# Moving the cross-attention's memory products ahead of the state recurrence in a hybrid encoder layer

## The chip, the cores and the metric

The kernel runs on one core of a Trainium2 chip. The metric is the device time of one execution in microseconds. The core has five engines with their own queues: PE (TensorE, matmuls and, as PEld, weight loads), DVE (VectorE), ACT (ScalarE), POOL (GpSimd) and SP (SyncE). In this kernel SP issues most of the DMAs and ACT the others.

## The reference

One layer of an encoder on x (2048 x 1024), with memory tokens mem (256 x 1024), all in float32:

```python
u = _rms_norm(h, norm_mix_g[l])
proj = u @ w_in[l]
hy = _short_conv_centred(proj[..., :HY_COLS], hy_conv_w[l], hy_conv_b[l])
spec = _hyena_filter_spectrum(L, ...)
y_hy = _group_rms_norm(_hyena(hy, spec, hy_skip[l]), hy_norm_g[l], HYENA_GROUPS)
qk = jax.nn.silu(_short_conv_centred(proj[..., HY_COLS:off], ml_conv_w[l], ml_conv_b[l]))
y_ml = _mlstm_bidirectional(qk[..., :D_MLSTM], qk[..., D_MLSTM:], v, o, gates, ml_gate_b[l])
y_ml = _group_rms_norm(y_ml, ml_norm_g[l], MLSTM_HEADS)
h = h + jnp.concatenate([y_hy, y_ml], axis=-1) @ w_out[l]
h = h + _cross_attention(_rms_norm(h, norm_x_g[l]), _rms_norm(mem, norm_mem_g[l]),
                         xa_wq[l], xa_wk[l], xa_wv[l], xa_wo[l])
h = h + jnp.square(jax.nn.relu(_rms_norm(h, norm_ff_g[l]) @ ff_w1[l])) @ ff_w2[l]
return _rms_norm(h, final_norm_g)
```

`_hyena` applies two long convolutions one after the other, each by a transform, a product with the filter's spectrum and an inverse transform over all 2048 positions. `_mlstm_bidirectional` is a recurrence over chunks of the sequence, once forwards and once backwards, for four heads of 128; the carried state of a head is a 128 x 128 matrix and a vector of 128.

## The kernel before

**Products in three parts.** A float32 product is made of three fast ones (`mm3`, L340 to L342): each operand is split into a rounded part and a remainder (`split`, L345: a cast on ACT, a subtraction on DVE). Weights come through `weights` (L374 for blocks of 256 columns, L369 for blocks of 1024): 256 KB land in a staging tile `wn` (three of these), are split into `wh` and `wl` (two of each), and `stream` keeps one item of the list `self.items` loading ahead. Each item is 1 MB.

**The input projection.** `w_in` is taken in ten blocks of 256 columns with the columns on the partitions (`sweep`: products of 512 positions, then the short convolution, then a transpose back) and in four blocks with the positions on the partitions (`natural`: products of 256 columns). Both walk over two halves of the sequence, `hf` 0 and 1. Blocks 0 and 1 of `natural` are v, blocks 2 and 3 are the output gate, block 3 also holds the 16 gate columns. Results go to DRAM (`hy`, `qt`, `kt`, `kn`, `vd`, `od`, `gt`).

**The convolution.** `hyena` first transforms z (`f1`), then for each of the two convolutions runs 16 frequency blocks (L845 the filter's response, L918 the transform, L876 the way back) and eight steps of the inverse transform (L177 and L188 side by side through `beside`, with `e2`), in the second convolution followed by the group norm on POOL and DVE and the store `yh`. It reads and writes its intermediate values in DRAM (`zs`, `zg`).

**The memory products.** Attention's queries and keys, and its values and output matrix, are joined beforehand: `memproj` makes, for each of eight items (four heads of xa_wk, four of xa_wv), a projection of mem (`project`, products of 256 columns), and from it either `keys` (with a 1 MB block of xa_wq, into `gd`) or `values` (with a block of xa_wo, into `vw`). mem's operand lies in four tiles `mt` that `prep_mem` fills.

**The states.** The backward recurrence needs a state ahead of each chunk of 128: `backward` makes 15 of them, from chunk 15 down. A step (`update`) scales v by the gate weights (POOL, L1078, tile `ve`), multiplies it with k (TensorE, L1082), adds the decayed old state (DVE, L1088, tile `cb`) and stores it to `cbd` (L1107); k and v come by L1064 and L1070. Each of these loads and stores is 256 KB. `far_states` makes the first eight inside the convolution, in a small pool with one `ve` and two `cb`; `mlstm` loads the eighth back (`old_state`, L1094) and makes the other seven in its own pool, then goes through the 16 chunks forwards (scores L1175, products with v L1213 and with the states L1215, and the forward update, L1082 again with DVE as its engine). At its start it loads the gate rows (L1142, eight DMAs).

**The order.** Everything is written as generators that yield a rough weight, and `weave(a, b, wa, wb)` lets two of them advance in proportion. `among` puts one step of a second generator after every so many of the first. The list of `program` is:

```python
weave(p.hyena(hs),
      chain(s, p.sweep(range(4, 10), 1, True), p.natural(1, (3, 0, 1, 2), lambda: p.prep_x(0)),
            p.natural(0, (3,)), among(p.sweep(range(4, 10), 0, False), p.gates(), 3),
            among(chain(p.natural(0, (0, 1), p.prep_mem, 2), take(n, 5)), p.far_states(), 1)),
      279, 499)
m = p.mlstm(ms)
weave(n, take(m, 13), 85, 75)
```

`n` is `memproj`. A scheduler with its own timing then sets each engine's queue from this order and from priorities; some instructions are pinned with `keep_in_program_order`. Each engine runs its queue in order. Pools are stacked, and a pool's space is given on only when its last readers are done.

Of the kernel before, what the change touches and what calls it, by code (L numbers as in the profile page):

```python
# [10 lines left out]
F32 = mybir.dt.float32  # L11
# [9 lines left out]
D = 1024  # L21
# [112 lines left out]
class Prog:  # L134
# [247 lines left out]
            cur = nxt  # L382
        yield cur

    NAT_AT = {0: 2}

    def inproj_open(self, es):
        nc, tc, a = self.nc, self.tc, self.a
        self.d_hy = self.dram("hy", (3, L, CH))
        self.d_qt = self.dram("qt", (4, 128, L))  # L390
        self.d_kt = self.dram("kt", (4, 128, L))
        self.d_kn = self.dram("kn", (L, CH))
        self.d_vd = self.dram("vd", (L, CH))
        self.d_od = self.dram("od", (L, CH))
        self.d_gt = self.dram("gt", (L, 16))
        sb = self.isb = es.enter_context(tc.tile_pool(name="i_sb", bufs=1))
        self.xh = sb.tile([128, 8, 1024], F32R, name="xh")
        self.xl = sb.tile([128, 8, 1024], F32R, name="xl")
        small = sb.tile([128, 448], F32, name="small")
        self.carry = small[:, 0:340].rearrange("p (c t) -> p c t", c=20)  # L400
        self.rx, self.rm = small[:, 340:356], small[:, 356:358]
        win = a["w_in"][0]
        tr = [(win[:, 256 * c:256 * c + 256], 256) for c in range(10)]
        nat = [(win[:, 2560 + 256 * c:2816 + 256 * c + 16 * (c == 3)], 256 + 16 * (c == 3)) for c in range(4)]
        hs = [slice(256 * h, 256 * h + 256) for h in range(4)]
        first = [(a[w][0][:, h], 256) for w in ("xa_wk", "xa_wv") for h in hs]
        second = [(a["xa_wq_t"][h, :], 1024) for h in hs] + [(a["xa_wo"][0][h, :], 1024) for h in hs]
        mem = first[:1]
        for i in range(8):
            mem += ([nat[self.NAT_AT[i]]] if i in self.NAT_AT else []) + first[i + 1:i + 2] + second[i:i + 1]  # L410
        items = tr[:4] * 2 + tr[4:] + [nat[c] for c in (3, 0, 1, 2, 3)] + tr[4:] + nat[:2] + mem
        self.items = items

    def inv_rms(self, dst, src):
# [166 lines left out]
    def prep_x(self, hf):  # L581
        self.prepq = chain(self.x_chunk(2 * hf), self.x_chunk(2 * hf + 1))

    def prep_mem(self):
        sb = self.isb
        self.memt = [[sb.tile([128, 1088], F32R, tag=tag, name="mt", bufs=2)[:, 0:D].rearrange("p (k t) -> p k t", k=4)
                      for tag in ("P", "cv")] for h in range(2)]

        def load(h):
            t = sb.tile([128, D], F32, tag="xn", name="xt", bufs=2).rearrange("p (k t) -> p k t", k=4)  # L590
            self.nc.sync.dma_start(out=t, in_=self.a["mem_t"].rearrange("(k p) t -> p k t", p=128)[:, 4 * h:4 * h + 4])
            return t

        def halves():
            xs = [load(h) for h in range(2)]
            rb = self.spread(self.diagonal(self.rm))
            for h in range(2):
                self.scaled(xs[h], 4 * h, self.g_mem, rb, *self.memt[h])
                yield
        self.prepq = halves()  # L600

    def memproj(self):
        nc, sb = self.nc, self.isb
        gd = self.dram("gd", (2, 128, 8, 512))
        vw = self.dram("vw", (4, 128, 8, 256))
        self.pop(2)
        mt = self.memt

        def project():
            wh, wl = next(self.wst)  # L610
            p = self.mm().rearrange("p (k t) -> p k t", k=2)
            for m in range(2):
                ms = slice(128 * m, 128 * m + 128)
                for k in range(8):
                    self.mm3(p[:, m], wh[:, k, ms], wl[:, k, ms], mt[k // 4][0][:, k % 4], mt[k // 4][1][:, k % 4], k == 0, k == 7)
            t = sb.tile([128, 2, 2, 256], F32R, tag="xn", name="kt", bufs=2)
            self.split(t[:, 0], t[:, 1], p)
            return t

# [25 lines left out]
                    o = staged(p.rearrange("p (i t) -> p i t", i=2))  # L645
                    nc.scalar.dma_start(out=vw[2 * d:2 * d + 2, :, 2 * h + mt].rearrange("i p c -> p i c"), in_=o)

        t = project()
        for i in range(8):
            if i in self.NAT_AT:  # L650
                yield from self.natural(0, (self.NAT_AT[i],))
            yield 11
            nxt = project() if i < 7 else None
            (keys if i < 4 else values)(i % 4, t)
            t = nxt

    def sweep(self, cols, hf, first, after=None):
        nc, a, sb = self.nc, self.a, self.isb
# [429 lines left out]
                nc.vector.scalar_tensor_tensor(new[:, h], old[:, h], DC[:, r + h:r + h + 1],  # L1088
                                               pc[:, 129 * i:129 * i + 129], ALU.mult, ALU.add)

    def old_state(self, sb, n):
        t = sb.tile([128, 4, 129], F32, tag="cf", name="cb", bufs=3)
        cbd = self.dram("cbd", (15, 128, 516))
        self.nc.sync.dma_start(out=t.rearrange("d h e -> d (h e)"), in_=cbd[n - 1])  # L1094
        return t

    def backward(self, sb, first, last, old, pin=None, lean=False):
        kn = self.dram("kn", (L, CH)).rearrange("(n s) c -> s n c", s=128)
        cbd = self.dram("cbd", (15, 128, 516))
# [8 lines left out]
            old = new  # L1108
        yield 3

    def far_states(self):
        with self.tc.tile_pool(name="m_b", bufs=1, side="right") as sb:
            yield from self.backward(sb, 15, 7, None, self.tc.keep_in_program_order, True)

    def mlstm(self, es):
        nc, tc, a = self.nc, self.tc, self.a
# [22 lines left out]
        for s in range(2):  # L1139
# [1 line left out]
            for q in range(4):  # L1141
                nc.sync.dma_start(out=t[32 * q:32 * q + 32], in_=by_half[s])  # L1142
# [721 lines left out]
def chain(*gens):  # L1864
    for g in gens:
        yield from g
# [20 lines left out]
def program(p):  # L1887
    with ExitStack() as ms:
        with ExitStack() as es:
            p.inproj_open(es)  # L1890
            p.filters_open()
            p.prepq = p.x_first()
            p.pop()
            s = chain(p.sweep(range(4), 0, True, lambda: p.prep_x(1)), p.sweep(range(4), 1, False))
            next(s)
            next(s)
            weave(s, p.filters(), 140, 80, True)
            p.gates_open(ms)
            n = p.memproj()
            with ExitStack() as hs:  # L1900
                weave(p.hyena(hs),
                      chain(s, p.sweep(range(4, 10), 1, True), p.natural(1, (3, 0, 1, 2), lambda: p.prep_x(0)),
                            p.natural(0, (3,)), among(p.sweep(range(4, 10), 0, False), p.gates(), 3),
                            among(chain(p.natural(0, (0, 1), p.prep_mem, 2), take(n, 5)), p.far_states(), 1)),
                      279, 499)
            m = p.mlstm(ms)
            weave(n, take(m, 13), 85, 75)
            for _ in take(m, 1):
                pass
        with ExitStack() as rs:  # L1910
            with ExitStack() as at:
                p.tail_open(at)
                g = p.attention(at)
                weave(g, m, 440, 96, True)
                ms.close()
                p.ffn_open(rs)
                for _ in g:
                    pass
            p.ffn()


def among(g, h, every):
# [45 lines left out]
```

## Time and profile before

| what | value |
|---|---|
| median of 3 runs | 3202.12 us (3199.16 to 3203.77) |
| the profiled execution, its own time | 3198.5 us |
| span of the profiled execution | 3196.7 us |
| PE busy | 3040.7 us (95%) |
| PEld busy | 2391.2 us (75%) |
| DVE busy | 2067.3 us (65%) |
| ACT busy | 1502.0 us (47%) |
| POOL busy | 1184.8 us (37%) |
| mean granted clock of TensorE | 0.982 |
| moved by DMA | 602.14 MB, mean 188 GB/s |

The page gives a busy time as a share of the whole span, and the ends of matmuls are modelled, so that neighbours overlap: a busy PE is not a PE at its peak. The stages have different limits, so the views by stretch say more than the totals. The profiled execution is one run, 3.6 us below the median.

### The profile page before, as it was taken

What the parts mean: (1) busy time and instruction counts of PE and PEld (TensorE: products, weight loads), DVE (VectorE), ACT (ScalarE), POOL (GpSimd) and SP (SyncE); (2) the same over time, 40 slices, a digit from 0 to 9 for tenths busy, and PEclk for the clock granted to TensorE, in tenths of its full rate; (3) what the DMA queues carried; (4) which work ended last, traced back from release to release, by engine and by line L of the source; (5) the groups of instructions that cost most, each with busy time, mean ns of one, the idle gap of its engine ahead of it and who ended that gap; (6) DMA issues with size and microseconds to landing.
All of it is one profiled execution on the core that took longest, in us unless ns stands there. A gap on an engine that the chain in (4) does not pass through costs nothing.

```text
span 3196.7 us, 43569 instructions
## 1 busy us (share of the span) xinstructions
PE 3040.7 (95%) x14473; PEld 2391.2 (75%) x14473; DVE 2067.3 (65%) x3563; ACT 1502.0 (47%) x2873; POOL 1184.8 (37%) x818
## 2 busy tenths in 40 slices
PE   6999999999999976999999998999999999999998
PEld 5655566776667766888878887888788878888876
DVE  7775366344874767877775547666655676555695
ACT  5543366424774344454444445555555443333335
POOL 0122012100121334324151218777766483434483
PEclk9999999999999988999999999999999999999999
DMA  5554766686677987556384437655544474444434
GB/s 186 196 198 168 252 195 209 171 266 197 170 231 209 300 269 236 171 169 207 108 295 150 162 120 243 210 195 188 193 153 157 147 248 156 139 135 149 125 93 168
DMA packets 445177, 602.14 MB, mean 188 GB/s; under 512 B 38670, under 2 KB 250766, under 8 KB 443928
## 3 DMA queue, kind: packets, MB, share of 16 engines
q1 hardware_dynamic: 406772, 540.84, 53.2%
q10 hardware_dynamic: 38180, 58.51, 5.5%
q8 instruction: 115, 1.88, 0.2%
q14 instruction: 110, 0.90, 0.1%
HBM read 401.00 MB, written 198.21 MB: 187 GB/s over the span
## 4 chain that ended last, share of the span: by engine, by line
PE 77%; DMA 9%; DVE 7%; issue 3%; ACT 2%; POOL 1%; SPq 1%; ACTq 0%; DVEq 0%; POOLq 0%
PE mm L340 16%; PE mm L341 16%; PE mm L342 16%; PE hy L342 5%; PE hy L340 5%; PE hy L341 5%; PE hy L177 3%; PE hy L876 2%; PE mm L845 1%; PE hy L918 1%; DVE bl L1540 1%; DVE wl L345 1%; PE hy L1082 1%; PE hy L1213 1%; DMA wn<-in_xa_wq_t_dram 1%
## 5 line engine op out<-in xcount | busy, mean ns | idle before, releaser
L345 DVE TENSOR_TENSOR wl<-wn,wh 128x512 fp32r<-128x512 f32 (+1 forms) x364 | 285.7, 820 | 115.8 <-ACT wh L345 115.8
L1540 DVE TENSOR_TENSOR bl<-wr,bh 128x512 fp32r<-128x512 f32 x213 | 236.3, 1115 | 130.8 <-ACT bh L1539 127.1
L345 ACT CAST wh<-wn 128x512 fp32r<-128x512 f32 (+1 forms) x364 | 208.2, 619 | 232.2 <-PE mm L342 56.2
L1539 ACT CAST ah<-w 128x512 fp32r<-128x512 f32 x284 | 176.2, 622 | 300.0 <-PE hy L341 152.1
L923 POOL TENSOR_TENSOR b<-b,a 128x512 f32<-128x512 f32 x64 | 87.8, 1372 | 582.0 <-ACT b L921 459.1
L340 PE MATMUL mm<-xh,wh 128*128 128x512 f32 x640 | 270.6, 424 | 4.5 <-ACT xh L500 2.3
L1540 DVE TENSOR_TENSOR al<-w,ah 128x512 fp32r<-128x512 f32 x236 | 228.6, 970 | 57.4 <-ACT ah L1539 56.9
L341 PE MATMUL mm<-xl,wh 128*128 128x512 f32 x640 | 257.1, 402 | 2.7 <-DVE xl L345 2.2
L342 PE MATMUL mm<-xh,wl 128*128 128x512 f32 x640 | 258.3, 404 | 0.0
L1539 ACT CAST bh<-wr 128x512 fp32r<-128x512 f32 x232 | 143.7, 621 | 235.7 <-PE mm L342 181.4
L342 PE MATMUL mm<-bh,al 128*128 128x512 f32 x576 | 224.0, 391 | 7.0 <-DVE al L1540 4.5
L340 PE MATMUL mm<-bh,ah 128*128 128x512 f32 x576 | 226.0, 392 | 1.7 <-DVE u L1666 1.6
L341 PE MATMUL mm<-bl,ah 128*128 128x512 f32 x576 | 225.1, 391 | 0.0
L341 PE MATMUL mm<-act,wh 128*128 128x512 f32 x512 | 200.5, 392 | 0.2 <-DVE act L345 0.2
L342 PE MATMUL mm<-act,wl 128*128 128x512 f32 x512 | 199.3, 391 | 0.0
L340 PE MATMUL mm<-act,wh 128*128 128x512 f32 x512 | 198.0, 393 | 0.7 <-ACT act L345 0.6
L1389 POOL TENSOR_TENSOR ssum<-ssum,sq 128x512 f32<-128x512 f32 x56 | 81.9, 1462 | 302.9 <-ACT sq L1388 302.9
L340 PE MATMUL hy<-bh,ah 128*128 128x512 f32 x448 | 175.2, 391 | 0.0
L341 PE MATMUL hy<-bl,ah 128*128 128x512 f32 x448 | 174.6, 390 | 0.0
L342 PE MATMUL hy<-bh,al 128*128 128x512 f32 x448 | 174.4, 390 | 0.0
L340 PEld LDWEIGHTS mm<-xh,wh 128*128 128x128 f32 x640 | 121.4, 190 | 65.4 <-issue 29.9
L323 POOL TENSOR_TENSOR b<-b 128x512 f32<-128x512 f32 x32 | 59.1, 1848 | 274.9 <-DVE P L685 126.4
(369 smaller groups left out, 8569.4 us busy)
## 6 DMA issues: line engine op xcount, KB each, us to landing
wr<-hc SPq DMA_DIRECT2D x224, 256.0 KB
w<-in_ff_w_dram SPq DMA_DIRECT2D x176, 256.0 KB
hc<-t SPq DMA_DIRECT2D x128, 256.0 KB
wn<-in_w_in_dram SPq DMA_DIRECT2D x100, 256.0 KB
hc<-q SPq DMA_DIRECT2D x96, 256.0 KB
fs<-a SPq DMA_DIRECT2D x32, 512.0 KB
a<-fs SPq DMA_DIRECT2D x64, 256.0 KB
a<-zs SPq DMA_DIRECT2D x64, 256.0 KB
```

Of the source, the lines that this page charges most:

```text
L177: b = self.nc.tensor.matmul(*products[-1], start=True, stop=True)
L323: nc.gpsimd.tensor_tensor(e[1], f, b, ALU.subtract)
L340: mm(ps, lh, rh, start=start, stop=False)
L341: mm(ps, lh, rl, start=False, stop=False)
L342: mm(ps, ll, rh, start=False, stop=stop)
L345: both = (self.nc.scalar.copy(hi, src), self.nc.vector.tensor_tensor(lo, src, hi.bitcast(F32), ALU.subtract))
L845: nc.tensor.matmul(pp, dm[:, m], t[:, m], start=True, stop=True)
L876: nc.tensor.matmul(pg, em[:, m], y, start=True, stop=True)
L923: nc.gpsimd.tensor_tensor(xt, xt, hi[:, m], ALU.mult)
L1389: nc.gpsimd.tensor_tensor(ssum, ssum, sq, ALU.add)
L1539: self.nc.scalar.copy(hi, src)
L1540: eng.tensor_tensor(lo, src, hi.bitcast(F32), ALU.subtract)
```

## The change

Six of the eight memory steps (all projections; keys of four heads, values of two) move from behind the convolution to its first half: a new helper `both` runs one step of `memproj` after every four steps of the sweep over the second half of the sequence, that is after each block of 256 columns. The projections for the last two values are kept in DRAM (`vt`) and read back later. mem's operand gets its own pool and is made at `memproj`'s first step. The list of weight items is reordered to fit. All 15 backward states are written down as part of the convolution's weave, beside and after `natural(0, (0, 1))`; `old_state` is gone. Behind the weave stand the last natural block, `natural(0, (2,))`, and the last two values, woven with the first steps of `mlstm`.

```diff
-        mem = first[:1]
-        for i in range(8):
-            mem += ([nat[self.NAT_AT[i]]] if i in self.NAT_AT else []) + first[i + 1:i + 2] + second[i:i + 1]
-        items = tr[:4] * 2 + tr[4:] + [nat[c] for c in (3, 0, 1, 2, 3)] + tr[4:] + nat[:2] + mem
+        mem = tr[4:6] + first[:1]
+        for i in range(4):
+            mem += [tr[6 + i], first[i + 1], second[i]]
+        mem += [first[5], second[4], first[6], second[5]]
+        items = tr[:4] * 2 + mem + first[7:] + [nat[c] for c in (3, 0, 1, 2, 3)] + tr[4:] + nat[:3] + second[6:]
...
-    def prep_mem(self):
+    def mem_operand(self, pool):
         sb = self.isb
-        self.memt = [[sb.tile([128, 1088], F32R, tag=tag, name="mt", bufs=2)[:, 0:D].rearrange("p (k t) -> p k t", k=4)
-                      for tag in ("P", "cv")] for h in range(2)]
+        self.memt = [[pool.tile([128, 4, 256], F32R, name=f"mt{x}{h}") for x in "hl"] for h in range(2)]
...
-        def project():
+        def pair():
+            return sb.tile([128, 2, 2, 256], F32R, tag="xn", name="kt", bufs=2)
+
+        def project(keep=None):
...
-            t = sb.tile([128, 2, 2, 256], F32R, tag="xn", name="kt", bufs=2)
+            if keep is not None:
+                nc.scalar.dma_start(out=vt[keep], in_=staged(p).rearrange("p i t -> p (i t)"))
+                return None
+            t = pair()
...
-        t = project()
-        for i in range(8):
-            if i in self.NAT_AT:
-                yield from self.natural(0, (self.NAT_AT[i],))
-            yield 11
-            nxt = project() if i < 7 else None
-            (keys if i < 4 else values)(i % 4, t)
-            t = nxt
+        with self.tc.tile_pool(name="m_t", bufs=1, side="right") as pool:
+            self.mem_operand(pool)
+            yield 0
+            t = project()
+            for i in range(6):
+                yield 11
+                nxt = project() if i < 5 else project(0)
+                (keys if i < 4 else values)(i % 4, t)
+                t = nxt
+            project(1)
+        yield 6
+        for i in range(2):
+            st = sb.tile([128, 512], F32, tag="st", name="st", bufs=3)
+            nc.sync.dma_start(out=st, in_=vt[i])
+            t = pair()
+            self.split(t[:, 0], t[:, 1], st.rearrange("p (i t) -> p i t", i=2))
+            values(2 + i, t)
+            yield 8
...
-    def far_states(self):
+    def back_states(self):
         with self.tc.tile_pool(name="m_b", bufs=1, side="right") as sb:
-            yield from self.backward(sb, 15, 7, None, self.tc.keep_in_program_order, True)
+            yield from self.backward(sb, 15, 0, None, self.tc.keep_in_program_order, True)
...
-        for _ in self.backward(sb, 7, 0, self.old_state(sb, 8)):
-            yield 3
...
-            n = p.memproj()
+            n, states = p.memproj(), p.back_states()
             with ExitStack() as hs:
                 weave(p.hyena(hs),
-                      chain(s, p.sweep(range(4, 10), 1, True), p.natural(1, (3, 0, 1, 2), lambda: p.prep_x(0)),
+                      chain(s, both(p.sweep(range(4, 10), 1, True), 4, n, 1, 8), p.natural(1, (3, 0, 1, 2), lambda: p.prep_x(0)),
                             p.natural(0, (3,)), among(p.sweep(range(4, 10), 0, False), p.gates(), 3),
-                            among(chain(p.natural(0, (0, 1), p.prep_mem, 2), take(n, 5)), p.far_states(), 1)),
-                      279, 499)
+                            both(p.natural(0, (0, 1)), 1, states, 2, 7), states),
+                      279, 530)
             m = p.mlstm(ms)
-            weave(n, take(m, 13), 85, 75)
-            for _ in take(m, 1):
-                pass
+            weave(chain(p.natural(0, (2,)), n), chain((12,), take(m, 6)), 38, 48)
...
+def both(g, n, h, m, rest):
+
+    h = take(h, rest)
+    for i, v in enumerate(g):
+        yield v
+        if i % n == n - 1:
+            yield from take(h, m)
+    yield from h
```

More of the change, by code (lines that the diff above doesn't have):

```diff
@@ L383, in stream @@
         yield cur
-    NAT_AT = {0: 2}
     def inproj_open(self, es):
@@ L592, in load @@
             return t
[L594 to L600, printed above, removed]
+        xs = [load(h) for h in range(2)]
+        rb = self.spread(self.diagonal(self.rm))
+        for h in range(2):
+            self.scaled(xs[h], 4 * h, self.g_mem, rb, *self.memt[h])
     def memproj(self):
@@ L605, in memproj @@
         vw = self.dram("vw", (4, 128, 8, 256))
-        self.pop(2)
-        mt = self.memt
-        def project():
+        vt = self.dram("vt", (2, 128, 512))
+        def pair():
+            return sb.tile([128, 2, 2, 256], F32R, tag="xn", name="kt", bufs=2)
+        def project(keep=None):
+            mt = self.memt
             wh, wl = next(self.wst)
@@ L1089, in update @@
                                                pc[:, 129 * i:129 * i + 129], ALU.mult, ALU.add)
[L1091 to L1095, printed above, removed]
     def backward(self, sb, first, last, old, pin=None, lean=False):
```

## Prediction

> **What bounds the kernel now.** I first read the slices of the page, to see where TensorE falls short of a full span.
>
> ```profile
> PE   6999999999999976999999998999999999999998
> PEclk9999999999999988999999999999999999999999
> DMA  5554766686677987556384437655544474444434
> ```
>
> TensorE is full nearly everywhere. Past the start, the only slices with a 7 and a 6 are the fifteenth and sixteenth (1119 to 1279 us). The granted clock falls there too, and DMA is at 7 to 9. So I read the busy time by stretches around them. The columns are the stretch, its length, the busy time and records of PE, PEld, DVE, ACT and POOL, then the PE clock, the DMA share and GB/s.
>
> ```profile
> 400.00:640.00 240.00, 233.40 (x1107) 171.65 (x1107) 140.12 (x214) 148.34 (x251) 43.35 (x32) 1.00 0.66 192
> 800.00:1018.00 218.00, 210.35 (x960) 150.38 (x959) 153.74 (x313) 143.79 (x238) 45.21 (x34) 1.00 0.69 199
> 1018.00:1080.00 62.00, 59.90 (x447) 51.90 (x447) 32.52 (x84) 17.68 (x36) 15.75 (x11) 0.97 0.92 278
> 1080.00:1140.00 60.00, 50.71 (x340) 40.17 (x336) 52.28 (x110) 24.33 (x45) 26.55 (x16) 0.97 0.92 287
> 1140.00:1172.00 32.00, 20.85 (x114) 18.26 (x112) 18.34 (x44) 14.73 (x33) 9.89 (x12) 0.86 0.74 233
> 1172.00:1216.00 44.00, 37.77 (x209) 32.69 (x210) 25.60 (x68) 15.62 (x32) 12.47 (x12) 0.91 1.00 327
> 1216.00:1273.00 57.00, 34.50 (x210) 31.57 (x210) 43.60 (x155) 21.98 (x91) 28.97 (x24) 0.75 0.66 216
> ```
>
> The first half of the convolution (400 to 640) leaves a third of the DMA time free and TensorE idles 6.6 us. From 1018 to 1216 the DMA engines are nearly full, because the second inverse transform and the memory products' weights come together, and TensorE waits. From 1216 to 1273 it waits for the mLSTM's own chain, with DMA at 0.66.
>
> A matmul's busy time is modelled to its end and neighbours overlap, so "busy" hides waiting. The step from one start to the next is the better price. In the time line of PE (start, duration):
>
> ```profile
> 1053.16 0.28 PE L340 MATMUL mm<-wh,xh 128*128 128x256 f32 x1
> 1053.29 0.28 PE L341 MATMUL mm<-wl,xh 128*128 128x256 f32 x1
> 445.13 0.39 PE L340 MATMUL mm<-xh,wh 128*128 128x512 f32 x1
> 445.36 0.39 PE L341 MATMUL mm<-xl,wh 128*128 128x512 f32 x1
> 1035.04 0.84 PE hy L177
> 1035.90 0.84 PE hy L177
> 1018.66 1.05 PE L1082 MATMUL hy<-ve,kn 128*128 128x129 f32 x8
> 1172.21 3.81 PE L1082 MATMUL hy<-ve,kn 128*128 128x129 f32 x16 [7.11 <-POOL ve L1078]
> 1198.30 1.05 PE L1082 MATMUL hy<-ve,kn 128*128 128x129 f32 x8
> 1205.40 1.02 PE L1175 MATMUL hy<-qn,kk_t 128*128 128x128 f32 x7 [0.20 <-DMA kk_t<-kt]
> 1216.29 1.05 PE L1082 MATMUL hy<-ve,kn 128*128 128x129 f32 x8
> ```
>
> So a product of 256 columns costs 0.12 us and one of 512 columns 0.23. A pair of the inverse transform costs 0.86, since L177 starts 0.86 apart and its partner L188 runs inside. A state of eight records costs 0.9. L1082 is the backward states up to 1198.30; at 1216.29 it is the forward update of the mLSTM's first chunk. I count the matmuls from the state at 1018.66 to that update, each kind by its own answer of the stretches: memory projections (tile mt), then kt (192 records of keys, the rest values), then the column products' third that reads xl, then the inverse transform's L177, then the states.
>
> ```profile
> 1018.66:1216.20 197.54, 57.26 (x384) 51.69 (x384) 0.00 (x0) 0.00 (x0) 0.94 0.91 284
> 1018.66:1216.20 197.54, 49.35 (x282) 40.41 (x282) 5.48 (x8) 4.64 (x8) 0.94 0.91 284
> 1018.66:1216.20 197.54, 21.90 (x77) 14.77 (x77) 0.00 (x0) 0.00 (x0) 0.94 0.91 284
> 1018.66:1216.20 197.54, 18.47 (x32) 3.85 (x32) 0.94 0.91 284
> 1018.66:1216.20 197.54, 17.18 (x104) 16.10 (x104) 0.94 0.91 284
> ```
>
> That is 384 x 0.12 = 46, keys 192 x 0.12 = 23, values 90 x 0.23 = 20.5, columns 3 x 77 x 0.12 = 27.7, sixteen pairs 13.8, thirteen states 11.6, and about 4.5 for the chunk itself: 147 us of matmuls in 197.5 us. **50.5 us are lost here, and they are what the change can win.**
>
> **The change, part by part.** TensorE's work is the same, only moved. *Out of the crowded stretch* go all eight projections (46), the four keys (23) and two of the four values (11): 80 us of matmuls, by the shapes in the code 14 MB of weights and 6 MB of results. In the changed order they lie between the columns of the first half. *Into their place* slide the last three groups of natural columns, which before had mostly run earlier. No removed operation leaves a gap by itself, so the gain is the 50.5 us less what is lost in three places.
>
> *First half of the convolution.* 192 GB/s over 240 us are 46 MB. With 20 MB more and about 5 MB of natural columns pushed out, it is 250 GB/s, between the rows at 192 and 278 that idle 2.7% and 3.4%. Lower bound: nothing, as the convolution's matmuls lie between a projection and its keys and cover the weights' casts. Upper bound: the 80 us idle as the row from 1080 does (9.3 of 60), 12 us. I take 4, near the row of 278, since the columns between have slack to load ahead. The memory operand itself (two loads, gains, two casts) moves into the filter stage, where TensorE is full; it costs nothing as long as that cover stands, and about 5 us otherwise.
>
> *Second inverse transform beside the columns.* The order shows some 93 us of matmuls: inverse pairs, three column groups, five states. Bounds: idle like the row from 1018 (2.1 of 62), 3 us; like the row from 1080, 14 us. It has less to load than either (columns take 1 MB per 23 us, memory products 1 MB per 6), but each state adds 0.75 MB. I take 7.
>
> *The end.* "All states while it runs" is not what TensorE's order says: ten of the fifteen states come after the last column product, six after everything else. Beside them stand 48 value products (11 us), two pairs (1.7) and then the first chunk: with ten states (9) 26 us of matmuls. The states are a chain. Before, its last seven, from 1172.21 to 1198.30, came 26.1 / 6 = 4.35 us apart. What makes a step:
>
> ```profile
> L1078 POOL TENSOR_TENSOR ve<-va,cols x15: 1041/1047/1299, 897.9 to 1193.0; 128x516 f32<-128x516 f32 x15
> L1088 DVE SCALAR_TENSOR_TENSOR cb<-cb,cols,hy x56: 334/342/350, 1001.1 to 1200.3; 128x129 f32<-128x129 f32 x56
> 1165.88 5.16 DMA va<-vd
> 1252.12 3.12 DMA va<-vd
> ```
>
> Now there is one ve buffer and two each of va, kn and cb. A load can be issued only when the state two before has let go: 1.05 (POOL) + 0.6 (issue) + 3.1 to 5.2 (landing), over two steps, is 2.4 to 3.4. SP is in order, and a kn load that waits for TensorE holds back the write and the loads behind it, among them the attention's first (six, queued between states). So 2.6 to 4.35; I take 3.9, near the measured chain, as the memory weights are gone from between the loads but the ve buffer is single. Nine steps: 35 us.
>
> After the last state the mLSTM opens. Its tiles take the space of the states' pool, so its first load waits for the last write to land. Before, near states, projections and values covered this opening; now nothing does.
>
> ```profile
> 1150.86 1.09 SPq L955 DMA_DIRECT2D yh<-a  x2
> 1155.95 7.67 SPq L1142 DMA_DIRECT2D rows<-rows  x8
> 1201.02 0.43 SPq L1149 DMA_DIRECT2D qn<-qt  x1
> ```
>
> Four DVE steps and the write's issue 1.7, landing 4 (the yh rows to the first rows load), eight row loads 5 to 7.7, qn's issue to the first score 4.4 (1201.02 to 1205.40), score to the chunk's update 10.9 before with values between, say 7: 23 us. The end takes 2 + 35 + 23 = 60 us for 26 us of matmuls: 34 lost. Bounds: 20 (steps of 2.6) to 42 (steps of 4.8).
>
> A clock that sinks belongs here.
>
> ```profile
> 1180.38 1.05 PE L1082 MATMUL hy<-ve,kn 128*128 128x129 f32 x8
> 1182.88 1.05 PE L1082 MATMUL hy<-ve,kn 128*128 128x129 f32 x8
> 1187.31 1.13 PE L1082 MATMUL hy<-ve,kn 128*128 128x129 f32 x8 [0.26 <-DMA kn<-kn]
> 1190.94 1.92 PE L1082 MATMUL hy<-ve,kn 128*128 128x129 f32 x8
> ```
>
> Of the seven states three took 1.9 us (two at 1172.21, one here) and four 1.05 to 1.13, at a clock of 0.91 over the stretch. The Trainium skill ("TensorE: Matmul & The Clock Gate", Part 1) says that an idle window of about 3.4 us halves TensorE's clock until it has been busy that long; the row agrees, and by that rule all of the end would run at half clock. That is the second rival below.
>
> *After the first chunk's update* the order on every queue is the same as before, so the 57 us from 1216 stay.
>
> **Sum.** -50.5 + 4 + 7 + 34 = -5.5 us against the profiled execution's 3198.5 us (span 3196.7), which is 3.6 below the median of 3202.1. I forecast the median at 3197.
>
> **The rivals.** 0.2% of this kernel, 6.4 us, is about what a measurement can tell from no change.
>
> 1. *The chain is fast.* With the crowd gone a load lands in 3.1 us as at 1252, steps take 2.6, and the inverse stage idles 3: -12 - 4, plus 2 of the first half's loss not taken: 3179 to 3184. For it: DMA was 1.00 where 4.35 was measured. Against: the order on SP. The Trainium skill ("DMA: Bandwidth & Descriptors", Latency and other measured facts) has HBM latency growing under load, which speaks for it; the two va rows agree.
> 2. *Cold end, slower than before.* TensorE has 26 us of work in 60. At half clock the states take 1.9 instead of 1.05 (steps of 4.8: +8), and values, pairs and scores lose about 5: +13, so 3210. It decides when the steps exceed 4.6 us, where the end's loss eats the remaining gain. For it: the clock of 0.75 from 1216 on. Against: four of the seven states kept the full clock.
> 3. *The crowd only moves.* A projection uses 1 MB in 6 us and keys the next; three staging tiles hold only 0.75 MB ahead. If each of the 14 steps waits about 1.3 us, with ACT at 0.62 of the first half already, the first half loses 18 instead of 4: 3211.
> 4. *Not what it says:* that ten states come late is in the forecast already.
>
> **Numbers.** Forecast (3190 to 3203) 0.42; rival 1, 0.22; rival 2, 0.21; rival 3, 0.15. Of the forecast's case not quite half is below 3195.7: with rival 1, faster 0.41. Slower takes most of rivals 2 and 3: 0.32. The rest, 0.27, is no change. The range leaves out the far ends of rivals 1 and 3: 3181 to 3214.
>
> **What would show it.** Right: first half idle under 5% with DMA near 250 GB/s; the last column product some 40 us earlier, against the first chunk's update, than TensorE's work there needs; ten L1082 groups about 4 us apart; a gap of about 20 us with few matmuls ahead of L1175's counterpart. Wrong: idle time beside projections and keys between 400 and 640; state steps under 3 or over 4.6; a first score within 10 us of the last state; or any change after the first chunk's update.

## The result, and the profile after

The changed kernel takes 3225.2 us in the median of 5 runs (3222.1 to 3228.3), the kernel before, run beside it, 3202.7 (3199.2 to 3204.9): a ratio of 1.0075 [1.0063, 1.0086]. The forecast was 3197, no change or a little faster; by the medians the change makes the kernel 22.5 us slower. The profiled execution has a span of 3226.6 us (own time 3228.3, the slowest of the five), 29.9 more than that of the kernel before, whose profiled execution lies below its median.

The slices of the changed kernel's page:

```profile
PE   7999999989999975999999999999999999999998
PEclk9999999989999986999999999999999999999999
```

The weak slices are still the fifteenth and sixteenth, now with a 7 and a 5 at a clock of 8 and 6, and a new one has come: the ninth (645 to 726 us) with an 8 and a clock of 8, where before stood a 9 in both rows. Stretches cut at the new places (columns as in the prediction), all of the changed kernel but the last, which is of the kernel before:

```profile
400.00:640.00 240.00, 237.71 (x1109) 173.65 (x1108) 160.26 (x241) 168.57 (x283) 42.90 (x32) 1.00 0.77 227
640.00:680.00 40.00, 25.26 (x110) 18.81 (x110) 10.42 (x20) 11.66 (x21) 0.00 (x0) 0.70 0.92 288
1060.00:1164.00 104.00, 97.09 (x707) 82.40 (x705) 61.74 (x148) 23.47 (x50) 33.24 (x24) 0.98 0.88 270
1164.00:1250.00 86.00, 39.05 (x174) 32.45 (x173) 37.01 (x114) 15.42 (x36) 28.06 (x27) 0.66 0.70 222
```
```profile
640.00:680.00 40.00, 37.96 (x264) 29.57 (x263) 10.78 (x20) 8.42 (x18) 0.00 (x0) 1.00 0.99 290
```

From 400 to 640 the memory products fit in with 2.3 us idle. From 640 to 680 TensorE idles 14.7 us (before 2.0), and what it does there runs at a clock of 0.70. The inverse stage, 1060 to 1164, idles 7. Then come 86 us with 39 us of busy time at a clock of 0.66: the end. In the time line of PE (the bracket is the idle time ahead and what ended it; left-out lines are matmuls between):

```profile
660.64 0.58 PE L340 MATMUL mm<-mth,wh 128*128 128x256 f32 x1 [7.88 <-ACT wh L345]
...
1170.39 0.80 PE L340 MATMUL mm<-wh,kt 128*128 128x512 f32 x1 [6.20 <-ACT kt L345]
...
1191.34 0.79 PE L340 MATMUL mm<-wh,kt 128*128 128x512 f32 x1 [7.66 <-ACT kt L345]
...
1200.70 1.05 PE L1093 MATMUL hy<-ve,kn 128*128 128x129 f32 x8
1202.99 1.16 PE L1093 MATMUL hy<-ve,kn 128*128 128x129 f32 x8 [1.24 <-POOL ve L1089]
1209.08 2.06 PE L1093 MATMUL hy<-ve,kn 128*128 128x129 f32 x8 [4.93 <-DMA kn<-kn]
...
1221.88 2.06 PE L1093 MATMUL hy<-ve,kn 128*128 128x129 f32 x8 [7.41 <-DMA kn<-kn]
1225.17 2.09 PE L1093 MATMUL hy<-ve,kn 128*128 128x129 f32 x8 [1.24 <-POOL ve L1089]
1242.34 2.05 PE L1178 MATMUL hy<-qn,kk_t 128*128 128x128 f32 x8 [15.07 <-DMA qn<-qt]
...
1250.52 1.10 PE L1093 MATMUL hy<-ve,kn 128*128 128x129 f32 x8
```

L1093 is the state's product (L1082 before), L1178 the scores. Two waits of 6.20 and 7.66 us stand ahead of the last two value products, and what they wait for is the split of the kept projections. Two waits of 4.93 and 7.41 stand ahead of states, for `kn`. Then come 15.07 us of opening. The waits of that stretch and SyncE's queue say why:

```profile
ACT kt L345 <- DMA st<-vt: 13.2, 2, 9.7
```
```profile
1164.94 0.55 SPq L662 DMA_DIRECT2D st<-vt  x1
...
1185.37 0.38 SPq L662 DMA_DIRECT2D st<-vt  x1
...
1203.88 0.65 SPq L1075 DMA_DIRECT2D kn<-kn  x1
...
1208.82 1.80 SPq L1347 DMA_DIRECT2D wn<-yh  x4
1210.67 1.02 SPq L1380 DMA_DIRECT2D acc<-in_x_t_dram  x2
1212.13 0.90 SPq L1075 DMA_DIRECT2D kn<-kn  x1
```

The kept projections are fetched only at 1164.9 and 1185.4, six microseconds or so ahead of their products. The attention's first six loads go out ahead of the `kn` of the state at 1221.88, which is issued at 1212.13 and used 9.8 us later. The `kn` of the state at 1209.08 was issued at 1203.88, before those loads, and used 5.2 us later, so the wait of 4.93 is not theirs.

The first forward update moved from 1216.3 to 1250.5, 34.2 us. Behind it the span is 1980.4 us before and 1976.1 after, and between 1976 and 1986 in the profiles of the experiments 1 to 8 as well, so these kernels differ ahead of this update. To compare stages I count as the prediction did: the start of an event in the trace less the matmuls queued ahead of it, at the prediction's prices. This *queue count* of lost time is, up to the convolution's last way-back and up to the first forward update:

(Each ratio is against runs of the kernel before on the same chip; there is no experiment 6. The counts come from one profiled execution of each kernel. Those of 5, 8 and 13 took 7 to 9 us more than their kernel's median. The changed kernel and experiments 1 to 3, whose first halves are written alike, stand between 67 and 74 at the way-back, so a difference of a few us in that column shows nothing. Only differences between rows are to be read: the prediction does not price every kind of matmul, and with each kind at its median step in the kernel before, the differences at the way-back come out up to 4 us smaller.)

| kernel | lost at way-back | lost at first update | first update at | ratio to before, 95% interval |
|---|---|---|---|---|
| before | 61 | 113 | 1216.3 | 1 |
| after | 74 | 146 | 1250.5 | 1.0075 [1.0063, 1.0086] |
| 1 states as before | 67 | 145 | 1250.2 | 1.0087 [1.0074, 1.0100] |
| 2 early reload | 71 | 132 | 1236.9 | 1.0044 [1.0032, 1.0056] |
| 3 loads behind | 70 | 137 | 1242.0 | 1.0068 [1.0056, 1.0080] |
| 4 steps spread | 69 | 129 | 1233.4 | 1.0036 [1.0024, 1.0049] |
| 5 = 2 + 3 + 4 | 74 | 122 | 1227.2 | 1.0004 [0.9993, 1.0014] |
| 7 states alone | 64 | 111 | 1213.0 | 1.0003 [0.9993, 1.0013] |
| 8 states under the sweep | 87 | 140 | 1244.9 | 1.0045 [1.0029, 1.0060] |
| 9 half moved | 61 | 108 | 1212.8 | 0.9979 [0.9970, 0.9989] |
| 10 filler | | | 1252.4 | 1.0076 [1.0059, 1.0092] |
| 11 half moved, 450 | 75 | 101 | 1201.3 | 0.9972 [0.9960, 0.9983] |
| 12 half moved, 430 | 83 | 102 | 1191.9 | 0.9931 [0.9917, 0.9944] |
| 13 nothing moved, 390 | 91 | 132 | 1203.4 | 0.9998 [0.9989, 1.0008] |

### The profile page after: what moved, and what is told of

Its sections match the earlier page's. It is cut to its first block, busy times and chain, and to the rows that moved or that the text cites. A ratio compares the mean times of both kernels' runs of the same rounds, so it can differ in the third digit from the quotient of the medians.

```text
span 3226.6 us, 43560 instructions
## 1 busy us (share of the span) xinstructions
PE 3053.4 (95%) x14473; PEld 2405.1 (75%) x14473; DVE 2062.7 (64%) x3563; ACT 1502.0 (47%) x2875; POOL 1180.1 (37%) x818
## 4 chain that ended last, share of the span: by engine, by line
PE 51%; DVE 4%; DMA 3%; issue 2%; POOL 1%; ACT 1%; SPq 1%; DVEq 0%; POOLq 0%; ACTq 0%
PE mm L342 11%; PE mm L340 11%; PE mm L341 11%; PE hy L342 5%; PE hy L340 5%; PE hy L341 5%; PE hy L1216 1%; PE hy L1218 1%; DVE bl L1543 1%; DVE al L1543 0%; PE hy L1093 0%; DMA w<-in_ff_w_dram 0%; PE hy L1464 0%; DVE wl L345 0%; DMA xs<-sm 0%
## 5 line engine op out<-in xcount | busy, mean ns | idle before, releaser
L345 DVE TENSOR_TENSOR wl<-wn,wh 128x512 fp32r<-128x512 f32 (+1 forms) x364 | 273.5, 788 | 124.6 <-ACT wh L345 124.1
L340 PE MATMUL hy<-xh,ah 128*128 128x512 f32 x384 | 153.0, 399 | 8.4 <-ACT ah L1542 7.7
```

The source lines that it names most:

```text
L340: mm(ps, lh, rh, start=start, stop=False)
L345: both = (self.nc.scalar.copy(hi, src), self.nc.vector.tensor_tensor(lo, src, hi.bitcast(F32), ALU.subtract))
```

## The experiments

**1 and 7: each half of the change alone.** Experiment 1 is the changed kernel with the states as before:

```diff
-            yield from self.backward(sb, 15, 0, None, ...)      # back_states
+            yield from self.backward(sb, 15, 7, None, ...)
+        for _ in self.backward(sb, 7, 0, self.old_state(sb, 8)):  # in mlstm, behind the gate rows
+            yield 3
-            weave(chain(p.natural(0, (2,)), n), chain((12,), take(m, 6)), 38, 48)
+            weave(chain(p.natural(0, (2,)), n), chain((12,), take(m, 14)), 38, 72)
```

> Undoes one part of the change: eight backward states beside the convolution and seven in the mLSTM, as before; the memory products stay in the first half. Theory 1 (the changed kernel lost its 28 us at four separate places: 13 us at the last memory steps, which have no columns between them; 14 us of waits for the kept projections' reload; 7 to 12 us of waits for state loads behind the attention's first loads; and about 25 us of uncovered mLSTM opening): the opening is covered again and the states shorten, but the 13 us at 640 to 680 us stay, and the reload still waits: 3205 to 3215. Rival theory 2 (the crowd is the loss: memory products cost their time in the first half wherever their surroundings lie): 3220 to 3230, states do not matter. Rival theory 3 (the states are the whole loss, the memory products' move is a gain): 3175 to 3200.

It came to 3226.8 us, the same as the changed kernel, so theory 1 missed and the range of theory 2 was met. Its first update comes at 1250.2 against 1250.5, though its states are placed quite differently. PE's time line of experiment 1:

```profile
1215.83 3.81 PE L1093 MATMUL hy<-ve,kn 128*128 128x129 f32 x16 [26.49 <-POOL ve L1089]
```

The opening is now ahead of the last seven states instead of behind all fifteen; TensorE waits 26.5 us at the one place instead of 15 at the other. Experiment 7 is the kernel before with the other half:

```diff
-            yield from self.backward(sb, 15, 7, None, ...)      # far_states
+            yield from self.backward(sb, 15, 0, None, ...)
-        for _ in self.backward(sb, 7, 0, self.old_state(sb, 8)):
-            yield 3
-            weave(n, take(m, 13), 85, 75)
+            weave(n, take(m, 5), 85, 51)
```

> The kernel before, with the states part of the change alone: all 15 backward states beside the convolution, memory products where they were. With the memory products alone (states as before) the time came out as that of the whole change, which theory 1 had not expected. Theory 4, formed from that: the loss is the end of the stretch, a chain of loads, states and mLSTM opening of some 85 us, which the memory products had covered and nothing covers now. Then states alone cost nothing, since projections and values still lie beside and behind them: 3190 to 3203. Rival theory 3 (states in a row in the small pool are themselves the loss): 3210 to 3225.

3201.4 us, a ratio of 1.0003: nothing. So the whole loss comes with the memory products, and moving the states neither costs nor gains. In experiment 7 values lie over the opening, and its bracket ahead of the first scores is 2.38 us:

```profile
1203.30 2.04 PE L1173 MATMUL hy<-qn,kk_t 128*128 128x128 f32 x8 [2.38 <-DMA vw<-o]
```

**10: is the end's length TensorE's work?**

```diff
+        filler = self.hy()
+        for _ in range(40):
+            tc.keep_in_program_order(nc.tensor.matmul(filler[:, 0:128], self.ident, self.ident, start=True, stop=True))
         scores(0, ld[0])
```

> The changed kernel with 40 more matmuls of 128x128 (8.7 us at 0.218 each, their result unused) pinned between the last state and the first scores, where the trace shows 15 us without a matmul. Theory 4 (the opening is loads and vector work, TensorE only waits): no change from 3225 (3222 to 3228), although TensorE does 8.7 us more. Cold clock as the cause (the rival of the prediction): the filler keeps TensorE busy, the scores and the first chunks run at the full clock, 3215 to 3221. If TensorE's work sets the end: 3232 to 3236.

```profile
1229.55 10.88 PE L1193 MATMUL hy<-ident 128*128 128x128 f32 x80
1243.98 2.05 PE L1178 MATMUL hy<-qn,kk_t 128*128 128x128 f32 x8 [3.56 <-DMA cbn<-cbd]
```

The filler's 10.9 us lie wholly in the gap and the ratio stays 1.0076. TensorE's work does not set the length of this stretch: 10.9 us of work that loads nothing are free there. That the memory products, which load weights too, had been as free over it in the kernel before is argued from this, not shown.

**2, 3 and 4: the waits one by one.** Experiment 2 fetches and splits the two kept projections between the first half's two v blocks, ahead of the crowded part of the queue:

```diff
-            nc.sync.dma_start(out=st, in_=vt[i])
-            t = pair()
-            self.split(t[:, 0], t[:, 1], ...)
-            values(2 + i, t)
+            self.tc.keep_in_program_order(nc.sync.dma_start(out=st, in_=vt[i]))
+            ts.append(pair())
+            self.split(ts[i][:, 0], ts[i][:, 1], ...)
+        yield 0
+        for i in range(2):
+            values(2 + i, ts[i])
...
-  both(p.natural(0, (0, 1)), 1, states, 2, 7), states),
+  both(p.natural(0, (0,)), 1, states, 2, 4), take(n, 1), both(p.natural(0, (1,)), 1, states, 2, 3), states),
```

> The two kept projections are reloaded and split while the second half's natural columns run, ahead of the crowded queue, and their value products find them ready. Theory 1: the waits of 6 and 7.7 us ahead of the two value products go and nothing takes their place: 3211 to 3217. Rival (the chain of states, issued beside them, ends the stretch anyway, so the waits are only idle time off the chain): 3222 to 3228.

3214.3 us, ratio 1.0044, within theory 1's range: of the two waits' 13.9 us about 10 come back. States still wait for `kn`, the longest 6.11 us. Experiment 3 queues the attention's first loads behind the opening's:

```diff
+        self.mark = self.last_v.ins        # the opening's last v load
...
+            with tc.issue_after(self.mark):
                 nc.sync.dma_start(out=yn, in_=src[...])
+                with tc.issue_after(self.mark):
                     nc.sync.dma_start(out=acc[:, 4 * h:4 * h + 4], in_=src)
```

> The attention's first six loads (3 MB, issued between the last states at 1208.8 to 1211.7 us) are queued behind the mLSTM's opening loads. Theory 1: the last four states no longer wait 4.9 and 7.4 us for kn: 3213 to 3219. Rival (the transfers have to be made somewhere and the opening's own loads then share with them, or the attention waits): 3223 to 3230.

3220.3 us. By the medians that is 5 us less than the changed kernel, but the intervals 1.0068 [1.0056, 1.0080] and 1.0075 [1.0063, 1.0086] overlap: by the times it is undecided, and 3220.3 lies between the ranges of both theories. In its trace the first update comes 8.5 us earlier, and of the last four states three follow without a wait for `kn`. The wait ahead of the first of them has stayed, as it must if the attention's loads did not make it:

```profile
1206.88 2.06 PE L1093 MATMUL hy<-ve,kn 128*128 128x129 f32 x8 [6.95 <-DMA kn<-kn]
1210.18 2.09 PE L1093 MATMUL hy<-ve,kn 128*128 128x129 f32 x8 [1.24 <-POOL ve L1089]
1213.51 2.09 PE L1093 MATMUL hy<-ve,kn 128*128 128x129 f32 x8 [1.24 <-POOL ve L1089]
1216.84 2.09 PE L1093 MATMUL hy<-ve,kn 128*128 128x129 f32 x8 [1.24 <-POOL ve L1089]
```

Steps of 3.3 us, with every product at 2.09, the slow length. So when the loads have landed the chain goes at 3.3 us even so; at 1200.70 to 1202.99 of the changed kernel, with products of 1.05 and 1.16, it is 2.3. The changed kernel's steps, 5.7 on average, were made longer than that by the waits, not by the clock.

Experiment 4 spreads the last memory steps over the natural columns:

```diff
-  mem += [first[5], second[4], first[6], second[5]]
+  mem += [nat[3], first[5], second[4], nat[0], first[6], second[5], nat[1], first[7], nat[2]]
...
-  both(p.sweep(range(4, 10), 1, True), 4, n, 1, 8), p.natural(1, (3, 0, 1, 2), ...),
+  both(p.sweep(range(4, 10), 1, True), 4, n, 1, 6), both(p.natural(1, (3, 0, 1, 2), ...), 2, n, 1, 3),
```

> The last memory steps, which follow one another without columns at 640 to 680 us, are spread over the natural columns of the other half (two columns' steps to each memory step). Theory 1: the idle 13 us of that place shrink to 2 to 4 and the end is untouched: 3212 to 3218, with TensorE busy over 38 of 40 us at 640 to 680. Theory 2 (the crowd only moves with the steps): 3222 to 3230, the idle time appears 40 us later. Theory 3 (only the states matter): the time shows no change from 3225.

3212.8 us, within theory 1's range, but only half for its reason. Stretches of experiment 4:

```profile
400.00:640.00 240.00, 231.39 (x1062) 168.74 (x1060) 156.13 (x236) 165.03 (x277) 42.95 (x32) 0.98 0.77 228
640.00:680.00 40.00, 36.47 (x232) 31.99 (x232) 9.39 (x21) 11.13 (x24) 0.00 (x0) 0.89 0.74 227
```

The 14.7 us idle at 640 to 680 become 3.5, but 6.3 more are idle ahead of 640, so 38 of 40 was not reached. At the way-back the queue count is 69, against 74 in the changed kernel and 61 before: at most 5 of the 13 us came back there, and that is no more than kernels with like first halves differ by. The other 12 us of the count were won at the end, where the scheduler's order also changed: the last inverse step stands at 1157 instead of 1183, and six states instead of five lie among the columns. This run doesn't tell what the spread itself is worth.

**5: the three repairs together.**

> The three repairs at once: kept projections reloaded early, attention's first loads queued behind the mLSTM's opening loads, last memory steps spread over columns. If the three places are separate, the gains add: 11 + 5 + 12.5 off 3225, 3197 (3193 to 3200). If one chain sets the end (theory 4), what is taken from one of its waits shows in another, and it stays at 3203 to 3209. A result under 3190 would mean that the places hinder one another.

3202.1 us, 1.0004: the kernel before is reached again, and not passed. The time lies between the two ranges. The gains in ratio (0.0031, 0.0007 and 0.0039, together 0.0077) add up within the intervals (0.0071), but not at the places meant: the way-back count is 74, as in the changed kernel, so by its profile the whole gain lies at the end and none in the first half. The end of experiment 5, from its last column product to its first update:

```profile
1165.20:1227.10 61.90, 34.35 (x161) 29.80 (x159) 29.17 (x91) 13.77 (x33) 22.55 (x23) 0.64 0.74 228
```

It takes 62 us where the changed kernel takes 86, at the same low clock (0.64 and 0.66): the idle time fell from 47 to 28 us. By the same measure it takes 74 us in experiment 2, 81 in 3 and 74 in 4. What is left in experiment 5 is above all the opening: 25.5 us from the last state (1201.7) to the first update (1227.2).

**8: more cover by the columns.** The v columns of the first half go ahead of the last sweep, whose blocks run k before q, so that six states are written beside its k blocks and the rest beside its q blocks and behind; reload and spread steps as in 2 and 4.

```diff
-  p.natural(0, (3,)), among(p.sweep(range(4, 10), 0, False), p.gates(), 3),
-  both(p.natural(0, (0,)), 1, states, 2, 4), take(n, 1), both(p.natural(0, (1,)), 1, states, 2, 3), states),
+  p.natural(0, (3, 0, 1)), among(p.sweep((4, 5), 0, False), p.gates(), 2),
+  both(p.sweep((8, 9), 0, False), 1, states, 1, 6),
+  both(p.sweep((6, 7), 0, False), 1, chain((0, 0), take(states, 6)), 1, 8), take(n, 1), states),
```

> The changed kernel with early reload and spread memory steps, and the v columns of the first half moved ahead of the last sweep, whose blocks run k before q, so that states start under the sweep; the last natural block, the inverse transform and the last two values now lie over the states and the mLSTM's opening, and one state instead of ten comes after the last column product. Theory 4 (cover decides): the end loses some 25 to 35 us less than in the changed kernel, with the spread 12 more: 3172 to 3190, faster than both. Rival theory 2 (DMA crowd: state loads beside the last sweep and the inverse transform slow these by what the end gains): 3200 to 3215.

3216.5 us: theory 4's number missed, the rival's nearly met. The queue count loses 87 up to the last way-back, 13 more than the changed kernel, and the states do not come early. In POOL's time line of experiment 8 they stand between the inverse transform's group norm (L962, L968):

```profile
1140.42 3.52 POOL L968 TENSOR_TENSOR a<-a,ghy 128x512 f32<-128x512 f32 x2 [3.21 <-DVE a L966]
1143.90 2.05 POOL L1093 TENSOR_TENSOR ve<-va,cols 128x516 f32<-128x516 f32 x1
1147.59 1.90 POOL L962 TENSOR_TENSOR a<-a 128x1024 f32<-128x1024 f32 x1 [1.64 <-PE mm L342]
```

A state's scaling (1 to 2 us) waits in order behind norms that wait for TensorE and DVE, and ten states take the 74 us from 1140 to 1214. That POOL's order is a reason is read from these lines; no run took it away. It is not the only one: ahead of the last two scalings POOL itself stood idle, 7.39 and 3.44 us, waiting for the state before. The reload also came late here (SyncE issued it at 1191), so this kernel isn't a clean trial of cover.

**9, 11, 12 and 13: move only what has a place.** Experiment 9 leaves the four key steps in the first half, one behind each column block, and makes the four value steps at the end as before, with all states in the convolution:

```diff
-  both(p.sweep(range(4, 10), 1, True), 4, n, 1, 8), ...
-  both(p.natural(0, (0, 1)), 1, states, 2, 7), states), 279, 530)
+  both(p.sweep(range(4, 10), 1, True), 4, n, 1, 6), ...       # projections and keys of four heads
+  both(p.natural(0, (0, 1), p.prep_mem, 2), 1, states, 2, 7),
+  both(chain(p.natural(0, (2,)), take(n, 1)), 1, states, 3, 9), states), 279, 552)
-  weave(chain(p.natural(0, (2,)), n), chain((12,), take(m, 6)), 38, 48)
+  weave(n, chain((12,), take(m, 5)), 38, 42)                   # projections and values of four heads
```

> Half of the change: the four key steps (four projections, four keys) stay in the first half, one behind each of the sweep's column blocks, where the changed kernel's trace idles nothing; the four value steps (four projections, four values) are made at the end as in the kernel before, beside the states, all fifteen of which are written into the convolution as in the changed kernel. Theory 4 (cover): the crowded stretch loses about half its 8 MB of weights, the first half loses under 3 us instead of 13, and the end keeps 45 us of matmuls over the states and the opening: 3175 to 3190, faster than both. Theory 2 (every memory step in the first half costs its share): 3200 to 3212.

3192.5 us, 0.9979: faster than before, but between the two ranges, by less than theory 4 expected. The half in the first half is free (61 lost at the way-back, as before); the end still waits 15.77 us ahead of its first scores. Experiments 11 and 12 change the one number 552 to 450 and 430, so that the convolution is written down ahead and the products lie behind it:

> The half-moved kernel with one number changed, the share of the other work in the convolution's weave (552 to 450): the convolution is written down faster against the columns, so that its last inverse step stands some 45 us of TensorE work earlier, the states lie between the last columns and the projections, one state alone comes behind them, and 12 us of products lie over the mLSTM's opening. Theory 4 (cover at the end is what is missing; the half-moved kernel still waits 15.8 us before its first scores): first scores follow the last state's opening with products between, 3178 to 3188. Rival theory 2 (DMA: the convolution's own loads then collide with the last sweep and it loses there what the end gains): 3192 to 3205.

> The same with 430: all states but none stand ahead of the last projection, and the first chunk lies among the last products. Theory 4: 3172 to 3185, at least as fast as with 450. Rival theory 2: slower than with 450, 3195 to 3210, with the loss beside the last sweep.

3190.3 and 3177.2 us; 11 missed theory 4's range by 2 us, 12 met it. Stretches of experiment 12, and its first scores:

```profile
1060.00:1164.00 104.00, 100.06 (x790) 96.75 (x789) 57.67 (x156) 29.38 (x59) 27.42 (x22) 0.97 0.71 221
1164.00:1250.00 86.00, 68.66 (x440) 61.89 (x439) 71.17 (x200) 47.38 (x147) 39.89 (x33) 0.92 0.91 298
```
```profile
1178.75 1.66 PE L1197 MATMUL hy<-qn,kk_t 128*128 128x128 f32 x8 [4.77 <-DMA qn<-qt]
```

The same 86 us that held 39 us of busy time in the changed kernel hold 69, the clock is 0.92 instead of 0.66, and 4.8 us instead of 15.1 stand ahead of the first scores. The first half pays for it (83 lost at the way-back), less than the end gains. The span is 24.8 us shorter than before: 11 of it by the first update (102 against 113), the rest behind it, where products lie beside the first chunks. Is it the number alone? Experiment 13 is experiment 7 with 499 lowered to 390:

> Control for the fastest kernel (half moved, 430): the states-only kernel, in which all memory products stay behind the convolution as before, with the share in the weave lowered by the same ratio (499 to 390). If the order of convolution, states and opening alone makes the gain: 3172 to 3182, as fast as with the half moved. If moving the key steps matters too (they take 4 MB of weights and 3 MB of results out of the end, and the first half took them in at no loss): 3184 to 3196.

3199.4 us, 0.9998: no, and above both ranges. Without the key steps moved this order gains nothing; the kernel loses 91 at the way-back already. Of the shares tried (552, 450 and 430 with the half moved, 499 and 390 without) the best is 430 with the half moved, 0.69% over the kernel before; no other share was run without the move.

## Why the prediction was wrong, by its own steps

- **The 50.5 us to win, and the inverse stage at 7:** right in size. The queue count puts 52 between the way-back and the first update of the kernel before, and the inverse stage lost 7 by the stretch from 1060 to 1164.
- **First half at 4:** mis-sized and in the wrong place. I spread the loss evenly and set the bounds by rows of other stages. Where a column block stands beside each memory step nothing is lost (237.7 of 240); where the last steps follow each other without columns, 640 to 680, 12.7 us more are idle than before. The order of TensorE showed those steps; I did not read it for the first half. The queue count gives 13 for the whole first half, so the upper bound of 12 holds nearly. That columns between the steps would have saved it is not shown: with columns there, experiments 4 and 5 still stand at 69 and 74 at the way-back. Experiment 9, with four steps only, stands at 61, as before.
- **The end at 60:** the failed step; it took 86. Its three parts were 2, 35 and 23. They came to 9.6 (1164.2 to the state at 1173.8), 51.4 (ten states, 1173.8 to 1225.2) and 25.3. What the sum lacked were waits for loads: 6.20 and 7.66 for the reload of the kept projections, to which it gave no term at all, and 7.41 for a `kn` behind the attention's loads, which I had named among the states without giving them a price. A fourth wait, 4.93 for a `kn`, is not the attention's; its like stays in experiment 3 (6.95). That the four make 26.2 us, just the missing 26, is partly chance: the state part holds 20.0 of them and is only 16.4 over, as its other steps were shorter than the 3.9 forecast. The experiments say how much the waits are worth: the end of 86 us became 74 with the reload made early (2) and 81 with the attention's loads behind (3), 17.5 of the 26 together. With the order of experiment 4 added it was 62 (5), which is near the 60 forecast; which wait that order took away is open. (The lower bound of 20 should have been 22: nine steps of 2.6 instead of 3.9 are 12 less than 34.)
- **-50.5 + 4 + 7 + 34** becomes -50.5 + 12.7 + 7 + 60 = 29, against 29.9 measured in the spans and 22.5 in the medians. The close agreement with the spans is luck in part, as the 12.7 counts idle time alone.
- **Rivals.** The crowd that only moves (3) came in part, at one place. The cold end (2) decided "when the steps exceed 4.6"; they took 5.7, but at the slow length the chain needs 3.3 when its loads are there (3). The low clock is real: the last four states and the two scores alone are about 1 us longer each. It isn't the 26, for the end of experiment 5 has the same clock and takes 62 us. I had no rival for "loads queued behind loads".
- **Signs.** Stated as right: idle under 5% and DMA near 250 in the first half (227 up to 640, then 288 with 37% idle, against it), the last column product some 40 us earlier than TensorE's work needs (86 us for 26 of work: 60), states about 4 us apart (5.7), a gap of about 20 us ahead of the scores (from the state's end at 1227.3 to 1242.3, 15). Stated as wrong: idle beside projections and keys between 400 and 640, which came just past that stretch; steps over 4.6, which came; a first score within 10 us of the last state and a change behind the first update (1980 and 1976 us), which did not come.
- Two of my later theories fell as well: that near states would cover the opening (1), and that v columns ahead of the sweep would (8).

## What to carry to other kernels

Work taken out of a crowded stretch may be the only thing that hides a chain of loads there. Before moving it, add up that chain (here states, opening and first scores, 62 us with the three repairs and 86 as first queued) and leave as much work over it; move only as many steps as the new place takes in without loss, here four of the eight. A value parked in DRAM costs TensorE no work, but its reload takes a place in a queue of loads, and that place must be priced: here two waits of 6.20 and 7.66 us.

## What the runs showed of the hardware

Stretches of experiment 10: the filler's first 3.8 us, its rest, and the scores behind it:

```profile
1229.60:1233.40 3.80, 3.80 (x20) 3.80 (x20) 0.67 (x3) 0.00 (x0) 0.21 (x2) 0.52 0.18 72
1233.80:1240.40 6.60, 6.60 (x60) 6.43 (x58) 1.18 (x4) 0.91 (x1) 0.52 (x2) 1.00 0.42 138
1243.90:1246.00 2.10, 2.02 (x8) 1.78 (x8) 0.52 (x2) 1.26 (x5) 2.10 (x2) 0.50 1.13 325
```

The granted clock is 0.52 for the first 3.8 us of the filler and 1.00 for the rest of it. Then TensorE stood 3.56 us, the clock was 0.50 again, and the scores took 2.05 us instead of the 1.16 of the next chunk's eight in the changed kernel:

```profile
1252.45 1.16 PE L1178 MATMUL hy<-qn,kk_t 128*128 128x128 f32 x8 [0.83 <-DVE cf L1095]
```

So a filler that ended 3.56 us early didn't keep the clock, and experiment 10 does not say what the opening would take at the full clock. The Trainium skill ("TensorE: Matmul & The Clock Gate", Part 1) puts the idle window at about 3.4 us, and this row agrees. In the states of experiment 3, idle gaps of only 1.24 us between products of 2.09 did not bring the full clock back over four states, 12 us; TensorE was busy for some six tenths of that time.
